# A hybrid attention layer on one core: PSUM banks, one engine's additions, paces and rings in six small edits

## The chip, the core and the metric

The kernel runs on one core of a Trainium2 chip. The metric is device time in microseconds (us) of one execution. Three runs of the kernel before gave 2157.15, 2158.1 and 2159.87 us, median 2158.1 us.

## The reference, cut to what matters

All in float32, 2048 tokens of 1024 features, behind 16 meta tokens:

```
xn = rms_norm(h);  proj = xn @ w_in                    # 6400 columns
sb_q, sb_k, sb_v, sw_q, sw_k, sw_v, sb_z, sw_z, g_sb, g_sw = split(proj)
o_sb = stick_breaking_attention(sb_q, sb_k, sb_v)      # 8 heads of 64, all earlier tokens
o_sw = sliding_window_attention(rope(sw_q), rope(sw_k), sw_v, sinks)   # 16 heads, 2 kv heads, window 128
y_sb = (o_sb * silu(sb_z)) @ w_branch_sb
y_sw = (o_sw * silu(sw_z)) @ w_branch_swa
h = h + (sigmoid(g_sb) * y_sb + sigmoid(g_sw) * y_sw) @ w_out
out = rms_norm(h) * final_norm_gain
```

Stick-breaking weights are products of `1 - sigmoid(score)` along the keys. The kernel forms them as a running product (a scan on VectorE) and takes differences of values in place of differences of weights.

## The kernel before

Each float32 operand of a large product is split into a high part and a low remainder (both of the type float32r), and a product is three matmuls: high by high, low by high, high by low. Tokens go in four groups of 512 (`g`), handled as two halves: groups 2 and 3, then 0 and 1 (the tokens are stored in reverse).

The stages of a half: **window**, in which the main stream on TensorE projects 128 columns at a time (`col_tile`, `gemm`, L403 to L405) while a side stream (`attend`) does the window attention; **stick**, in which the main stream projects gates (sigmoid on ScalarE, L567) while the side stream (`stick`) does stick-breaking; then the last gates. After both halves **finish** does the branch projections (`project`, L223 to L225), the merge, the output projection (L282 to L284) and the final norm.

TensorE's instructions are in the order of the code. `weave` sets how main and side alternate: each piece of the main stream gives credit by a `ratio`, and each piece of the side stream yields its cost. `SR` (L32) multiplies the window's ratio; a yield of 0.45 (L932) is the price of one stick row. The other engines' order, and that of the DMA queue on SyncE (SP), is made by the framework's scheduler, save at the start, where some of them are written out by hand.

PSUM is held in named rings of banks: `g` 2, `z` 2, `t` 2, `zm` 1, `o` 1. SBUF scratch comes from rings too: `tmp` (7 tiles of 128x512), and in finish `a` (6), `R` (32) and `L` (32).

In `stick`, `row` makes scores in `z` (and `zm`, for the block that holds the meta keys), takes a sigmoid on ScalarE (L869), masks on GpSimd (L871), and scans on VectorE (L873). `turn` transposes finished weights into `t` (L886), and `evac_split` copies them out: ScalarE the high part (L112), then VectorE the remainder (L113). `turn_meta` does the same for the meta keys through `zm` (L896), and ScalarE copies the high part there once more (L899). `values` accumulates a head's output in `o` (L915), 128 rows, of which the two halves are to be added. At the end of a head and group ScalarE copies 64 rows to `tmp` (L919), and VectorE adds the other 64 from the bank (L920). The meta keys' product stays in `zm` (L911) until VectorE has added it for a pair of heads (L922).

In `window`, `rope` rotates a projected tile: four copies of 32 rows on ScalarE (L627, L628), two products on VectorE (L629, L630), and their sum on GpSimd (L631). `put_k` and `put_q` split the result (L639 to L641, L688, L689). The attention's turned weights are split by L112 and L113, masked on GpSimd (L741), multiplied in `o` (L754), and added up by L756 and L760. Its exponentials are L716.

Helpers named below: `firsts` (L528) turns the first column of each value tile, through `zm`; `meta_cols` (L426) turns a small meta tile, by default through `zm`; `sb_k`'s `later` first loads such a tile from DRAM (`msd`) and then turns it through `t`. `split` makes high and low weights (L108 on GpSimd, L109 on GpSimd or VectorE). `gated` loads two tiles, multiplies them (L197), and splits the product (L199 ScalarE, L200 VectorE). In finish, `out_weights` loads and splits a tile of `w_out` (L234, L235).

Of the kernel before, what the change touches and what calls it, by code (L numbers as in the profile page):

```python
# [31 lines left out]
SR = 1.05  # L32
# [12 lines left out]
def tile_kernel(ctx, tc, x, xt, meta, metat, gain, w_in, w_sb, w_sw, w_out, sinks, fgain,  # L45
# [146 lines left out]
    def gated(src, zz, k, g, ring, stg):  # L192

        a, b = stg(), stg()
        DMA(a, src[k][g])
        DMA(b, zz[k][g])
        V.tensor_tensor(a, a, b, op=ALU.mult)  # L197
        h, l = ring(), ring()
        A.copy(h, a)  # L199
        V.tensor_tensor(l, a, f32(h), op=ALU.subtract)  # L200
        return h, l

    def finish(ringl, osw, first):
# [6 lines left out]
        def ringr(dt=F32R):  # L210
            return cp.tile([P, GT], dt, tag="R", name="ringr", bufs=32)
# [5 lines left out]
        DMA(fg, fgain.to_broadcast([P, D]))  # L217

# [8 lines left out]
        for half, groups in enumerate(halves):  # L227
            part, merged, wo = {}, {}, {}

            def out_weights(k, ch):  # L230
                raw = small("a", AB)
                DMA(raw, w_out[0, k * P:(k + 1) * P, ch * GT:(ch + 1) * GT])
                h, l = wo[k, ch] = ringr(), ringr()
                A.copy(h, raw)  # L234
                V.tensor_tensor(l, raw, f32(h), op=ALU.subtract)  # L235
# [4 lines left out]
            for d, g in order:  # L240
                if d == 4 and g == groups[0]:
                    if half == 0:
                        cp.tile([P, 48], F32, name="padr")
                    osb = {(k, g): gated(od, zs, k, g, ringr, lambda: small("a", AB)) for g in groups for k in range(4)}
# [7 lines left out]
                part[d, g] = ringr(F32)  # L252
# [14 lines left out]
            for g in groups:  # L267
                for t0 in range(0, 4, 2):
                    res, ssq = {}, {}
                    end = (half, g, t0) == (1, groups[1], 2)  # L270
                    for ch in range(2):
                        cs = slice(ch * GT, (ch + 1) * GT)
                        for t in (t0, t0 + 1):
# [25 lines left out]
                    for t in (t0, t0 + 1):  # L299
# [23 lines left out]
                if half == 0:  # L323
                    g2 = halves[1][g - groups[0]]
                    osw2.update({(k, g2): gated(ow, zw, k, g2, ringl, lambda: small("a", AB)) for k in range(8)})
# [111 lines left out]
    spare = [False]  # L437

# [4 lines left out]
    def sb_k(p):  # L443
        def use(g, acc, ms):
# [4 lines left out]
            if ms is not None:  # L449
                def later():  # L450
                    if p < 2:
                        t = tp.tile([NM, P], F32, tag="ms", name="ms", bufs=2)
                        DMA(t, msd[p])
                    mc = meta_cols(t if p < 2 else ms, "t" if p < 2 else "zm")
# [45 lines left out]
    def sb_v(p):  # L500

        def use(g, acc, ms):
# [22 lines left out]
            def firsts():  # L525

                tr = ps("zm")
# [75 lines left out]
    def window(half, groups, sp):  # L603
# [20 lines left out]
        def rope(acc, c, s, t, u, scale):  # L624
# [6 lines left out]
            G.tensor_tensor(t, t, u, op=ALU.add)  # L631
# [14 lines left out]
        def sw_k():  # L646
            def use(g, acc, ms):
# [142 lines left out]
    def stick(groups, bp, sums_of={}):  # L790
# [102 lines left out]
        def turn_meta(h, g):  # L893
            tr = ps("zm")
# [4 lines left out]
            A.copy(w[64:96], tr[:32])  # L899
            av_todo.append((h, g, vm[:, h // 2, :], w, None, False, False))  # L900

        def values():
# [6 lines left out]
            if wl is None:  # L909
                st["m"] = ps("zm")  # L910
# [334 lines left out]
```

## Time and profile before

| what | value |
|---|---|
| median of three runs | 2158.1 us |
| the profiled execution's own time | 2158.47 us |
| its span, first to last instruction | 2156.8 us |
| VectorE busy | 1359.7 us (63%) |
| ScalarE busy | 1025.2 us (48%) |
| GpSimd busy | 376.2 us (17%) |
| GB/s over the span | 176 |

A row of a group reads: line, engine, operation, tiles written and read, shape, count, then busy time and mean duration, then the idle time of that engine before these instructions and what ended it. A row of the waits reads: engine, tile and line, what it waited for, total, number of times, longest. PE is TensorE, PEld its weight load, DVE VectorE, ACT ScalarE, POOL GpSimd.

### The profile page before, as it was taken

The page shows a single profiled execution, that of the slowest core. Times are in us where ns is not written, and L with a number is a line of the kernel's source. Part 1 is how long each engine was busy: PE and PEld are TensorE (multiplying, and loading weights), DVE is VectorE, ACT ScalarE, POOL GpSimd, SP SyncE. Part 2 cuts the span into 40 slices and gives each one's busy share as a digit, 9 for nine tenths or more (in the row PEclk, how much of TensorE's full clock was granted, in tenths as well). Part 3 has the DMA queues.
Part 4 walks back from the last instruction along what each step waited for, and adds up shares of the span by engine and source line. Part 5 has one row for each costly group of instructions (what it writes and reads, how often), then busy time and mean ns, then how long its engine had stood idle before and what let it go on. Part 6 is the DMA issues. An engine that isn't in the chain of part 4 may idle for free.

```text
span 2156.8 us, 30229 instructions
## 1 busy us (share of the span) xinstructions
PE 2118.4 (98%) x10534; PEld 1754.4 (81%) x10534; DVE 1359.7 (63%) x2121; ACT 1025.2 (48%) x2456; POOL 376.2 (17%) x490
## 2 busy tenths in 40 slices
PE   8899999999999999999999999999999999999998
PEld 7778887888888888888887888888888888787887
DVE  7787876465545443777746888878775446454453
ACT  6576775344444434777744555555554201221121
POOL 2233343323223200222310000000000232000000
PEclk9999999999999999999999999999999999999999
DMA  9755454755655464444355333323322985468532
GB/s 339 257 181 196 157 188 165 261 192 202 200 189 179 163 226 156 147 167 138 136 183 175 118 118 117 117 88 119 119 84 99 353 315 186 160 223 295 161 103 88
DMA packets 174520, 380.40 MB, mean 176 GB/s; under 512 B 22720, under 2 KB 40960, under 8 KB 174368
## 3 DMA queue, kind: packets, MB, share of 16 engines
q1 hardware_dynamic: 174368, 378.48, 52.2%
q8 instruction: 83, 1.36, 0.3%
q14 instruction: 69, 0.57, 0.1%
HBM read 237.35 MB, written 140.98 MB: 175 GB/s over the span
## 4 chain that ended last, share of the span: by engine, by line
PE 86%; issue 4%; DVE 4%; ACT 3%; DMA 2%; POOL 1%; SPq 0%; POOLq 0%; ACTq 0%; DVEq 0%
PE ps_g L403 14%; PE ps_g L404 14%; PE ps_g L405 14%; PE ps_o L915 6%; PE ps_z L866 5%; PE ps_t L886 5%; PE ps_z L708 3%; PE ps_o L754 3%; PE ps_g L224 1%; PE ps_g L225 1%; PE ps_g L223 1%; PE ps_z L225 1%; PE ps_z L224 1%; PE ps_z L223 1%; PE ps_t L225 1%
## 5 line engine op out<-in xcount | busy, mean ns | idle before, releaser
L403 PE MATMUL ps_g<-xh,wh 128*128 128x512 f32 x1544 | 635.2, 411 | 7.4 <-ACT xh L967 6.9
L405 PE MATMUL ps_g<-xh,wl 128*128 128x512 f32 x1544 | 606.9, 393 | 0.6 <-DVE wl L109 0.6
L404 PE MATMUL ps_g<-xl,wh 128*128 128x512 f32 x1544 | 606.8, 393 | 0.0
L873 DVE TENSOR_TENSOR_SCAN row<-row 128x512 f32<-128x512 f32 (+2 forms) x320 | 374.7, 1173 | 178.8 <-POOL row L871 109.8
L405 PEld LDWEIGHTS ps_g<-xh,wl 128*128 128x128 f32 x1544 | 290.7, 188 | 66.3 <-DVE wl L109 1.1
L403 PEld LDWEIGHTS ps_g<-xh,wh 128*128 128x128 f32 x1544 | 291.8, 189 | 53.8 <-ACT xh L967 6.9
L404 PEld LDWEIGHTS ps_g<-xl,wh 128*128 128x128 f32 x1544 | 292.4, 189 | 43.4 <-DVE xl L968 1.3
L869 ACT ACTIVATE row<-ps_z 128x512 f32<-128x512 f32 (+2 forms) x320 | 164.9, 516 | 196.2 <-PE ps_z L866 193.3
L113 DVE SCALAR_TENSOR_TENSOR wtl<-ps_t,wth 128x512 fp32r<-128x512 f32 (+1 forms) x320 | 189.7, 593 | 43.2 <-ACT wth L112 42.1
L112 ACT ACTIVATE wth<-ps_t 128x512 fp32r<-128x512 f32 (+1 forms) x320 | 170.3, 532 | 71.1 <-PE ps_t L886 69.8
L866 PE MATMUL ps_z<-kt,q 128*128 128x512 f32 (+4 forms) x640 | 177.8, 353 | 0.4 <-ACT row L869 0.4
L886 PE MATMUL ps_t<-ident,row 128*128 128x128 f32 x1088 | 171.3, 272 | 1.3 <-DVE row L873 1.3
L886 PEld LDWEIGHTS ps_t<-ident,row 128*128 128x128 f32 x1088 | 136.1, 140 | 37.5 <-DVE row L873 1.7
L871 POOL TENSOR_SCALAR_AFFINE_SELECT row<-row 128x128 f32<-128x128 f32 x128 | 42.9, 336 | 628.6 <-ACT row L869 596.9
L866 PEld LDWEIGHTS ps_z<-kt,q 128*128 128x128 f32 x640 | 118.8, 188 | 24.1 <-ACT row L869 0.8
L915 PE MATMUL ps_o<-wth,vc 128*128 128x512 f32 (+1 forms) x320 | 126.0, 394 | 4.7 <-DVE xs L920 4.5
L108 POOL TENSOR_SCALAR wh<-raw 128x1024 fp32r<-128x1024 f32 (+1 forms) x63 | 68.6, 1089 | 303.1 <-PE ps_g L404 188.6
L716 ACT ACTIVATE sc<-sc,nm 128x129 f32<-128x129 f32 x256 | 100.0, 393 | 39.8 <-DVE nm L714 39.2
L567 ACT ACTIVATE tmp<-ps_g 128x512 f32<-128x512 f32 x112 | 67.0, 598 | 108.8 <-PE ps_g L405 99.0
L915 PE MATMUL ps_o<-wtl,vc 128*128 128x512 f32 (+1 forms) x320 | 116.5, 364 | 0.0
L109 POOL TENSOR_TENSOR wl<-raw,wh 128x1024 fp32r<-128x1024 f32 (+1 forms) x43 | 97.4, 2266 | 3.1
L631 POOL TENSOR_TENSOR tmp<-tmp 128x512 f32<-128x512 f32 (+1 forms) x37 | 48.7, 1316 | 201.7 <-DVE tmp L630 75.0
(309 smaller groups left out, 3411.7 us busy)
## 6 DMA issues: line engine op xcount, KB each, us to landing
wh<-h_in_w_in SPq DMA_DIRECT2D x66, 512.0 KB
wl<-l_in_w_in SPq DMA_DIRECT2D x66, 512.0 KB
raw<-in_w_in SPq DMA_DIRECT2D x50, 512.0 KB
h_in_w_in<-wh SPq DMA_DIRECT2D x50, 512.0 KB
l_in_w_in<-wl SPq DMA_DIRECT2D x50, 512.0 KB
q<-qd SPq DMA_DIRECT2D x128, 128.0 KB
vc<-vd SPq DMA_DIRECT2D x48, 256.0 KB
kd<-tmp SPq DMA_DIRECT2D x32, 256.0 KB
```

The costliest lines, as they stand in the source:

```text
L109: (V if vsplit[0] else G).tensor_tensor(l, src, f32(h), op=ALU.subtract)
L112: A.activation(h, acc, AF.Copy, scale=scale)
L113: V.scalar_tensor_tensor(l, acc, scale, f32(h), op0=ALU.mult, op1=ALU.subtract)
L403: T.matmul(acc, lhsT=wh[:, k, :], rhs=xh[g][:, k, :], start=k == 0, stop=False)
L404: T.matmul(acc, lhsT=wh[:, k, :], rhs=xl[g][:, k, :], start=False, stop=False)
L405: T.matmul(acc, lhsT=wl[:, k, :], rhs=xh[g][:, k, :], start=False, stop=k == KT - 1)
L716: A.activation(sc[:, hh, :], sc[:, hh, :], AF.Exp, bias=nm[:, hh:hh + 1], accum_out=den[:, hh:hh + 1])
L866: T.matmul(acc[:, :b - a], lhsT=lq, rhs=kt[h][:, k0 + a:k0 + b], start=t == 0, stop=t == 1)
L869: A.activation(r[:, a:b], acc[:, :b - a], AF.Sigmoid, scale=-1.0)
L873: V.tensor_tensor_scan(r[:, :w], r[:, :w], r[:, :w], last[j] if n else 1.0, op0=ALU.mult, op1=ALU.min)
L886: T.transpose(tr[:, j * P:(j + 1) * P], rows_of[h, g, n - (j > i), j][:, k0:k0 + P], ident)
L915: T.matmul(o[:, :n], lhsT=v, rhs=r, start=first and r is wh, stop=last and r is wl)
```

## The change

Six things change; the matmuls stay the same in number and shape.

1. **Banks of stick-breaking copied out at once.** ScalarE copies all 128 rows of `o`, and VectorE adds the two halves from that copy. The product in `zm` is copied to a `tmp` tile right behind its matmul.
2. **The rotation's sum** goes from GpSimd to VectorE.
3. **Turns in other banks.** `firsts`, `turn_meta` and the meta columns of the rotated keys use `t`; `turn_meta`'s second copy reads SBUF. The two `msd` tiles are loaded when the queue of held work is refilled, ahead of the function that turns them.
4. **Paces.** The window's factor is 1.05 in the first half and 1.09 in the second. The first six rows of stick-breaking cost 1.0 in place of 0.45. In the second half a one-column exponential stands behind the preparation of the last tokens.
5. **Finish's rings.** `R` becomes two rings of 16, one for the partial sums and the first column half of `w_out`, one for the gated values and the second half. The first four row blocks of each half go 3 and 1 in place of 2 and 2.
6. **Gating in two steps.** The remainder of one tile is taken behind the product of the next.

```diff
-SR = 1.05
+SR = (1.05, 1.09)
...
-    def gated(src, zz, k, g, ring, stg):
+    def gated(src, zz, keys, ring, stg):
...
+            V.tensor_tensor(a, a, b, op=ALU.mult)
+            h, l = out[k, g] = ring(), ring()
+            A.copy(h, a)
+            if rest:
+                V.tensor_tensor(rest[0], rest[1], f32(rest[2]), op=ALU.subtract)
+            rest = l, a, h
...
-        def ringr(dt=F32R):
-            return cp.tile([P, GT], dt, tag="R", name="ringr", bufs=32)
+        def ringr(n, dt=F32R):
+            return cp.tile([P, GT], dt, tag=f"R{n}", name="ringr", bufs=16)
...
-                h, l = wo[k, ch] = ringr(), ringr()
+                h, l = wo[k, ch] = ringr(ch), ringr(ch)
...
-                for t0 in range(0, 4, 2):
+                for ts_ in ((0, 1, 2), (3,)) if g == groups[0] else ((0, 1), (2, 3)):
...
+    def load_held():
+        for p in range(2):
+            held_ms[p] = tp.tile([NM, P], F32, tag="msh", name="msh", bufs=2)
+            DMA(held_ms[p], msd[p])
+        pending.extend(held)
...
-                tr = ps("zm")
+                tr = ps("t")
                 T.transpose(tr[:8, :P], vf[:, f0:f0 + 8], ident)
...
-            G.tensor_tensor(t, t, u, op=ALU.add)
+            V.tensor_tensor(t, t, u, op=ALU.add)
...
-                        rope(meta_cols(ms), cm, sm, t, u, 1.0)
+                        rope(meta_cols(ms, "t"), cm, sm, t, u, 1.0)
...
         def turn_meta(h, g):
-            tr = ps("zm")
+            tr = ps("t")
...
-            A.copy(w[64:96], tr[:32])
+            A.copy(w[64:96], f32(w[0:32]))
...
-                st["m"] = ps("zm")
-                T.matmul(st["m"], lhsT=v, rhs=wh, start=True, stop=True)
+                acc = ps("zm")
+                T.matmul(acc, lhsT=v, rhs=wh, start=True, stop=True)
+                st["m"] = tmp()
+                A.copy(st["m"], acc)
...
-                t, both = tmp(rows=64), pair(h, g)[1]
-                A.copy(t, o[64:128])
-                V.tensor_tensor(both[64 * a:64 * a + 64], o[0:64], t, op=ALU.add)
+                t, both = tmp(), pair(h, g)[1]
+                A.copy(t, o)
+                V.tensor_tensor(both[64 * a:64 * a + 64], t[0:64], t[64:128], op=ALU.add)
...
-                yield 0.45
+                yield 0.45 if s > LT else 1.0
...
+                A.activation(tp.tile([P, 4], F32, tag="nwt", name="nwt", bufs=2)[:, :1], xl[groups[1]][:, 0, 0:1], AF.Exp, scale=0.0)
                 drain(by_group(ts, groups[:1]), by_group(ts, groups[1:]))
...
-            weave(main, side, 4 * 2.15 / 20.8 * SR)
+            weave(main, side, 4 * 2.15 / 20.8 * SR[half])
```

Line numbers in the rows of the changed kernel are its own. **Start of stick-breaking in the second half, on TensorE.** Before, where L866 is a row's score matmul, L886 a turn, and L403 to L405 one step of the main stream's projection:

```order
L866 MATMUL ps_z<-kt,q_12181 128x512
L866 MATMUL ps_z<-kt,q_12182 128x512
L866 MATMUL ps_z<-kt,q_12181 128x512
L866 MATMUL ps_z<-kt,q_12182 128x512
L866 MATMUL ps_z<-kt,q_12181 128x512
L866 MATMUL ps_z<-kt,q_12182 128x512
L403 MATMUL ps_g<-xh,wh 128x512
L404 MATMUL ps_g<-xl,wh 128x512
L405 MATMUL ps_g<-xh,wl 128x512
L866 MATMUL ps_z<-kt,q_12181 128x512
L866 MATMUL ps_z<-kt,q_12182 128x512
```

In the changed kernel a score matmul is L876, and the projection L409 to L411:

```order
L876 MATMUL ps_z<-kt,q_12199 128x512
L876 MATMUL ps_z<-kt,q_12200 128x512
L409 MATMUL ps_g<-xh,wh 128x512
L410 MATMUL ps_g<-xl,wh 128x512
L411 MATMUL ps_g<-xh,wl 128x512
L876 MATMUL ps_z<-kt,q_12199 128x512
L876 MATMUL ps_z<-kt,q_12200 128x512
L409 MATMUL ps_g<-xh,wh 128x512
L410 MATMUL ps_g<-xl,wh 128x512
L411 MATMUL ps_g<-xh,wl 128x512
```

One projection step now stands between any two of the first rows; before, three rows stood in a line.

**End of stick-breaking in the second half, on TensorE.** Before, with the meta turn L896, the meta product L911 and the heads' products L915:

```order
L896 MATMUL ps_zm<-ident,xs 32x128 x4
L403 MATMUL ps_g<-xh,wh 128x512
L404 MATMUL ps_g<-xl,wh 128x512
L405 MATMUL ps_g<-xh,wl 128x512
L886 MATMUL ps_t<-ident,row 128x128 x4
L915 MATMUL ps_o<-wth,vc 128x512
L915 MATMUL ps_o<-wtl,vc 128x512
L403 MATMUL ps_g<-xh,wh 128x512
L404 MATMUL ps_g<-xl,wh 128x512
L405 MATMUL ps_g<-xh,wl 128x512
```

In the changed kernel the meta turn is L906, a turn L896, the meta product L921 and the heads' products L927:

```order
L906 MATMUL ps_t<-ident,xs 32x128 x4
L896 MATMUL ps_t<-ident,row 128x128 x4
L927 MATMUL ps_o<-wth,vc 128x512
L927 MATMUL ps_o<-wtl,vc 128x512
L927 MATMUL ps_o<-wth,vc 128x512
L927 MATMUL ps_o<-wtl,vc 128x512
L921 MATMUL ps_zm<-wm_71,vm 128x512
L927 MATMUL ps_o<-wth,vc 128x512
L927 MATMUL ps_o<-wtl,vc 128x512
L409 MATMUL ps_g<-xh,wh 128x512
```

The last turns and products now stand without projection steps between them.

**A head's end in the second half's stick-breaking, on ScalarE.** Before, L919 being the copy from `o`, L869 the rows' sigmoid, L112 the turned weights' high part:

```order
L112 ACTIVATE wth<-ps_t 128x512
L869 ACTIVATE row<-ps_z 128x512
L112 ACTIVATE wth<-ps_t 128x384
L567 ACTIVATE tmp<-ps_g 128x512
L919 COPY tmp<-ps_o 64x512
L869 ACTIVATE row<-ps_z 128x512
```

In the changed kernel L923 is the copy from `zm`, L931 the one from `o`, L879 the rows' sigmoid:

```order
L112 ACTIVATE wth<-ps_t 128x512
L879 ACTIVATE row<-ps_z 128x512
L112 ACTIVATE wth<-ps_t 128x384
L923 COPY tmp<-ps_zm 128x512
L931 COPY tmp<-ps_o 128x512
L879 ACTIVATE row<-ps_z 128x512
```

One more copy stands directly ahead of the one that empties `o`; the gate's sigmoid has moved away from there.

More of the change, by code (lines that the diff above doesn't have):

```diff
@@ L190, in rings @@
         return lambda dt=F32R: lp.tile([P, GT], dt, tag="L", name="ringl", bufs=32)
-    def gated(src, zz, k, g, ring, stg):
[L194 to L201, printed above, removed]
+    def gated(src, zz, keys, ring, stg):
+        out, rest = {}, None
+        for k, g in keys:
+            a, b = stg(), stg()
+            DMA(a, src[k][g])
+            DMA(b, zz[k][g])
+            V.tensor_tensor(a, a, b, op=ALU.mult)
[4 more added lines that the diff above has]
+            rest = l, a, h
+        if rest:
+            V.tensor_tensor(rest[0], rest[1], f32(rest[2]), op=ALU.subtract)
+        return out
     def finish(ringl, osw, first):
@@ L217, in finish @@
         DMA(fg, fgain.to_broadcast([P, D]))
+        small("gt", 3), ringr(0), ringr(1)
+        cp.tile([P, 48], F32, name="padr")
         def project(acc, ws, ox):
@@ L241, in finish @@
                 if d == 4 and g == groups[0]:
-                    if half == 0:
-                        cp.tile([P, 48], F32, name="padr")
-                    osb = {(k, g): gated(od, zs, k, g, ringr, lambda: small("a", AB)) for g in groups for k in range(4)}
+                    osb = gated(od, zs, [(k, g) for g in groups for k in range(4)], lambda: ringr(1), lambda: small("a", AB))
                 if d not in ws_of:
@@ L251, in finish @@
                 DMA(gt, gw[d][g])
-                part[d, g] = ringr(F32)
+                part[d, g] = ringr(0, F32)
                 V.tensor_tensor(part[d, g], acc, gt, op=ALU.mult)
@@ L324, in finish @@
                     g2 = halves[1][g - groups[0]]
-                    osw2.update({(k, g2): gated(ow, zw, k, g2, ringl, lambda: small("a", AB)) for k in range(8)})
+                    osw2.update(gated(ow, zw, [(k, g2) for k in range(8)], ringl, lambda: small("a", AB)))
             osw = osw2
@@ L450, in later @@
                 def later():
[L451 to L454, printed above, removed]
+                    mc = meta_cols(held_ms[p] if p < 2 else ms, "t" if p < 2 else "zm")
                     h, l = tmp(F32R)[:, :NM], tmp(F32R)[:, :NM]
@@ L1188, in tile_kernel @@
                     drain(tiles_by_tile([mk], groups))
[L1189 to L1190 removed]
+                osw.update(gated(ow, zw, todo[:4], ringl, tmp))
                 del todo[:4]
[L1192 to L1193 removed]
+            osw.update(gated(ow, zw, todo, ringl, tmp))
     first = weights(0, w_sw)
```

13 lines of the change are left out of this document (5 added, 8 removed).

## Prediction

> **What bounds the kernel now.** I read the page's first part, then TensorE's waits, then the timeline at each of them.
>
> ```profile
> PE 2118.4 (98%) x10534; PEld 1754.4 (81%) x10534; DVE 1359.7 (63%) x2121; ACT 1025.2 (48%) x2456; POOL 376.2 (17%) x490
> ```
>
> TensorE is the bound nearly everywhere, and the change leaves its 10534 matmuls alone. Only what it waits for can go:
>
> ```profile
> PE ps_g L403 <- ACT xh L967: 6.9, 1, 6.9
> PE ps_o L915 <- DVE xs L920: 4.5, 12, 0.8
> PE ps_zm L866 <- DVE xs L922: 2.8, 3, 1.4
> PE ps_zm L528 <- DVE vt L113: 2.7, 2, 1.7
> PE ps_zm L426 <- DVE vv L113: 2.3, 1, 2.3
> PE ps_o L754 <- DVE os L760: 2.0, 2, 1.0
> PE ps_t L426 <- DMA ms<-msd: 1.7, 1, 1.7
> PE ps_t L886 <- DVE row L873: 1.3, 2, 0.8
> PE ps_z L282 <- ACT ringr L234: 1.3, 1, 1.3
> ...
> PE ps_z L708 <- DVE sc L712: 0.6, 1, 0.6
> PE ps_g L223 <- ACT ringl L199: 0.6, 1, 0.6
> ...
> PE ps_g L403 <- DVE tmp L629: 0.4, 1, 0.4
> PE ps_z L866 <- ACT row L869: 0.4, 1, 0.4
> ```
>
> The first row is the load before the first matmul and stays. Each of the others here is a place that the change touches. A wait costs more than its idle time, as one in the timeline of the second half's stick-breaking shows:
>
> ```profile
> 1536.18 0.58 ACT L919 COPY tmp<-ps_o 64x512 f32<-64x512 f32 x1
> 1536.73 0.39 PE L404 MATMUL ps_g<-xl,wh 128*128 128x512 f32 x1
> 1536.80 0.68 DVE L920 TENSOR_TENSOR xs<-ps_o,tmp 64x512 f32<-64x512 f32 x1 [0.83 <-ACT tmp L919]
> 1536.96 0.40 PE L405 MATMUL ps_g<-xh,wl 128*128 128x512 f32 x1
> 1537.54 0.50 PE L915 MATMUL ps_o<-wth,vc 128*128 128x512 f32 x1 [0.18 <-DVE xs L920]
> 1537.87 0.40 PE L915 MATMUL ps_o<-wtl,vc 128*128 128x512 f32 x1
> ```
>
> Matmuls start 0.23 us apart (1536.73 to 1536.96). Here the next two starts are 0.58 and 0.33 later, 0.45 more than two steps, for 0.18 of idle time: each wait costs 0.27 us of refilling besides. I add that to every wait.
>
> **The change part by part**, against the profiled execution's 2158.47 us (0.4 above the median of the runs).
>
> *Banks copied out.* In these rows ScalarE has read its half of `o` at 1536.76, but TensorE, ready at 1537.19, waits for VectorE's addition until 1537.48. A copy of all 128 rows frees the bank at 1536.76, since one instruction takes 0.58 us by its 512 columns. So the 12 waits go: 4.5 + 12 x 0.27 = 7.7. `zm` is freed behind its matmul instead of behind L922: 2.8 + 3 x 0.27 = 3.6. Against that, in one head of two the new copy from `zm` (0.58 us like L919) stands ahead of the one from `o`, more than the margin of 0.43: 0.15 + 0.27 late, 0 to 16 times, so 0 to 6.7. VectorE's additions now hold nobody. The meta turn's place in `t` is priced by its own copies:
>
> ```profile
> 1650.82 0.60 PE L896 MATMUL ps_zm<-ident,xs 128*32 128x128 f32 x4
> 1651.46 0.59 ACT L112 ACTIVATE wm<-ps_zm 32x512 fp32r<-32x512 f32 x1 [1.00 <-PE ps_zm L896]
> 1652.08 0.68 DVE L113 SCALAR_TENSOR_TENSOR wm<-ps_zm,wm 32x512 fp32r<-32x512 f32 x1 [0.89 <-ACT wm L112]
> ```
>
> The bank is free 1.94 us after the turn began, and of two banks it is wanted two turns on; only where VectorE is late does anybody wait, 0 to 16 x 0.3 us. I take 0.5 for either: gain 11.3 - 1.0 = **10.3**.
>
> *Other turns.* `firsts` and the rotated meta keys no longer queue behind `zm`'s evacuation: 2.7 + 2.3 + 3 x 0.27 = 5.8. The longest of them, 2.3 us ending at 90.75, is followed by this:
>
> ```profile
> 91.00:94.50 3.50, 3.50 (x9) 2.68 (x10) 2.54 (x5) 1.91 (x7) 1.08 (x1) 0.54 1.03 421
> ```
>
> The granted clock is 0.54 for 3.5 us: 3.5 x 0.46 = 1.6 us lost, which goes with the wait. The Trainium skill (TensorE: Matmul & The Clock Gate, What's actually happening) has the clock halve after an idle window of about 3.4 us; by that, a wait of 2.3 us needn't be the cause, this 1.6 would stay, and the sum would be 1.6 smaller. The trace has the dip right behind the wait and behind none of the shorter ones, so I keep it. What takes the waits' place is VectorE:
>
> ```profile
> 112.00:160.00 48.00, 44.83 (x245) 37.37 (x244) 42.16 (x82) 36.69 (x109) 15.22 (x19) 1.00 0.52 176
> 160.00:360.00 200.00, 199.96 (x1076) 167.76 (x1074) 158.11 (x297) 138.36 (x409) 73.04 (x103) 1.00 0.51 177
> ```
>
> Between 112 and 160 it is busy 42.2 of 48 us, and both `firsts` waits lie there. With four rotation sums more (2.7 us) in 45 us it would be full, so half of these two waits (3.2 with refills) comes back: gain 5.8 + 1.6 - 1.6 = **5.8**.
>
> *Meta tiles loaded ahead:* 1.7 + 0.27, **2.0**. The two small loads stand one projected tile earlier in SP's queue, and TensorE doesn't want what is behind them there.
>
> *Rotation's sum.* What it replaces, its likeness on VectorE, and how the two engines meet:
>
> ```profile
> L631 POOL TENSOR_TENSOR tmp<-tmp 128x512 f32<-128x512 f32 (+1 forms) x37 | 48.7, 1316 | 201.7 <-DVE tmp L630 75.0 <-DMA qd<-tmp 71.1 <-ACT sc L711 16.1
> L630 DVE TENSOR_TENSOR tmp<-tmp,sn 128x512 f32<-128x512 f32 x14 | 9.6, 682 | 0.0
> 93.42 1.28 POOL L631 TENSOR_TENSOR tmp<-tmp 128x512 f32<-128x512 f32 x1 [7.10 <-DVE tmp L630]
> 93.45 1.27 DVE L630 TENSOR_TENSOR tmp<-tmp,mcs 128x16 f32<-128x16 f32 x1
> ```
>
> 37 sums of 0.68 us are 25 us for VectorE in place of 49 for GpSimd. The last two rows show what that buys back: a 16-column product lasts 1.27 us, as long as GpSimd's sum beside it. In 160 to 360 eleven sums bring VectorE from 79% to (158.1 + 7.5) / 200 = 83%, and TensorE waits nowhere there (199.96 busy). So the cost is 0 to 25 us; hidden while `z`, `g` and `t` are emptied in time. I take **-1**.
>
> *Paces.*
>
> ```profile
> 871.69 1.28 ACT L716 ACT_TABLE_LOAD   x1
> 1102.79 1.28 ACT L567 ACT_TABLE_LOAD   x1
> 1109.49 0.47 PE L754 MATMUL ps_o<-ph,vv 128*128 128x512 f32 x1 [0.95 <-DVE os L760]
> ```
>
> The exponential's table is loaded at 871.69, ahead of the first window unit; TensorE's waits for L712 and L629 follow. The early exponential takes it out of the way: 0.6 + 0.4 + 2 x 0.27 = 1.5. The load then stands in ScalarE's queue ahead of casts of the last tokens, to which TensorE comes three projections (3 x 24 x 0.23 = 16.6 us) later. At 1102.79 a gate's sigmoid comes between exponentials and costs a load; with 1.09 the side stream ends before the gates. But the first half has the same wait for L760 with no such load, so I count half of 0.95 + 0.27 plus small slips: 0.8. First rows one by one: L886 1.3, L866 0.4, three refills, 2.5; with one projection step to a row they come 5 x 0.23 = 1.15 us apart, and a row's turn follows five rows later, so these go. The 6 x 0.55 of pace come due at the end, where nothing is left between the last turns and products: TensorE has eight transposes and four products, about 1.8 us, between the meta turn's start and its product, which needs 0.64 + 0.59 + 0.58 for ScalarE's two copies at least and another 0.6 for the turn between them, and then the last turn's remainder. About 1.0 us in each half, 0 to 2. Sum 1.5 + 0.8 + 2.5 - 2.0 = **2.8**.
>
> *Finish.*
>
> ```profile
> 1845.93 8.49 SPq L55 DMA_DIRECT2D a<-in_w_out  x8
> 1852.03 1.93 ACT L234 CAST ringr<-a 128x512 fp32r<-128x512 f32 x3 [4.53 <-DMA a<-in_w_out]
> ```
>
> The second column half of `w_out` is asked for at 1845.93, converted from 1852.03, and wanted at 1851.25. Three row blocks ahead of it in place of two move the wish by 24 x 0.23 = 5.5 us: 1.3 + 0.27 = 1.6 go. The fourth block's input must wait for the first block's output, with six banks to cover that. Gating in two steps frees VectorE from ScalarE's copy, but that wait (0.6 + 0.27) hangs on DMAs in six `a` tiles: half, 0.4. **2.0.**
>
> Sum: 10.3 + 5.8 + 2.0 - 1 + 2.8 + 2.0 = 21.9; 2158.5 - 21.9 = 2136.6, less 0.4 for the median, **2136 us**. With nothing given back and every wait gone whole it is 11.3 + 7.4 + 2.0 + 5.2 + 2.5 = 28.4, so 2130.
>
> **The rivals.** *The finer edits miss* (0.12): the 1.09, the rings and the gating change no wait, and the clock dip stays: 2136 + 0.8 + 2.0 + 1.6 = 2140.
>
> *GpSimd holds the new additions* (0.13). In the first half's stick-breaking GpSimd is busy 29.5 of 100 us:
>
> ```profile
> 500.00:600.00 100.00, 100.00 (x516) 83.38 (x515) 57.71 (x73) 44.73 (x112) 29.45 (x30) 1.00 0.57 190
> 453.65 2.42 POOL L109 TENSOR_TENSOR wl<-raw,wh 128x1024 fp32r<-128x1024 f32 x1
> 453.79 3.36 DVE L873 TENSOR_TENSOR_SCAN row<-row 128x512 f32<-128x512 f32 x1
> ```
>
> The scan there takes 3.36 us beside GpSimd's 2.42. The 32 head sums read `o` and SBUF before; now they read SBUF twice, as the scan does. If each of the 16 of the first half that meet GpSimd were held for half of such a run, and TensorE waited for what stands behind, in 29.5% of the cases: 16 x 0.3 x 1.2 = 5.8, so 2142. The Trainium skill says so too (GPSIMD Engine Reference, Specifications): GpSimd's SBUF interfaces are shared with VectorE, which contends when it has two SBUF inputs. The rows agree.
>
> *The waits change their name* (0.14): `o` and `t` are then waited for behind ScalarE's longer queue and VectorE's remainders. The bounds above, 6.7 and 4.8 in place of 1.0, with the `firsts` waits back in full (1.6 more): 2136 + 10.5 + 1.6 = 2148.
>
> *No change* (0.07): that and the misses together, about 2154.
>
> *VectorE becomes the bound of the windows, slower* (0.04): every rotation sum delays an emptied bank by its 0.68 and a refill, 36 x 0.95 = 34: 2136 + 1 + 33 = 2170. It decides from where VectorE is full; 83% speaks against it, 112 to 160 for it.
>
> **How the numbers follow.** My forecast holds 0.50, from 2130 to 2139. The range takes in the next three cases, 2140 to 2148: 2130 to 2148. A measurement of this kernel tells 0.2%, 4.3 us, from none. Faster 0.50 + 0.12 + 0.13 + 0.14 = 0.89, the same 0.07, slower 0.04.
>
> **What would show it.** TensorE's waits should lack L920, L922, L528, L426 and the `msd` load, and the clock at 91 to 95 should be full. VectorE should be busy over 95% between 110 and 155. New waits of about a microsecond should stand at the two ends of stick-breaking. I am wrong if the windows show many short waits for L712, L629 or L113, or if `t` in stick-breaking does.

## The result and the profile after

The changed kernel takes 2136.47 us (median of four executions, 2134.13 to 2137.47) against 2157.7 us for the kernel before: a ratio of 0.9898, with a 95% interval of 0.9881 to 0.9915. That is 21.2 us less. The profiled execution took 2136.89 us with a span of 2135.0, so 21.8 us of span went. In the runs that follow, one execution of the kernel with fast first rows (2387 us) and one of the kernel before (2336 us) ran at a granted clock of 0.83 and 0.85, and the times given are medians without these two.

The page's row of busy time answers to the one shown of the kernel before: VectorE and ScalarE do a little more, GpSimd less, and TensorE the same 10534 matmuls in a shorter time.

```profile
PE 2112.2 (99%) x10534; PEld 1755.9 (82%) x10534; DVE 1383.4 (65%) x2158; ACT 1030.5 (48%) x2471; POOL 333.1 (16%) x453
```

TensorE's waits in the changed kernel (engine, tile and line, what it waited for, total us, times, longest). The lines have moved: L896 is now the turn in `t`, L921 and L927 are the products of stick-breaking in `zm` and `o`, L527 a turn of value tiles in `zm`, L232 a matmul of finish's projection, and L203 the deferred subtraction of gating.

```profile
PE ps_g L409 <- ACT xh L979: 7.0, 1, 7.0
PE ps_g L232 <- DVE ringl L203: 1.9, 1, 1.9
PE ps_o L409 <- ACT xh L383: 1.6, 1, 1.6
PE ps_t L896 <- DVE wtl L113: 1.2, 2, 0.6
PE ps_z L718 <- DVE q L699: 0.8, 2, 0.5
PE ps_o L927 <- DVE wtl L113: 0.7, 1, 0.7
PE ps_t L896 <- DVE wm L113: 0.7, 1, 0.7
PE ps_zm L527 <- DVE vt L113: 0.5, 1, 0.5
```

The twelve waits of `o` for an addition, the three of `zm`, those of `firsts`, of the rotated meta keys and for the `msd` load, and the ones in the window for a rotation are all gone. What is left is the load at the start, the wait at 66.9 us for the first group's tokens (it was 0.96 us before, and lies between nothing and 1.6 from kernel to kernel in what follows, without any edit near it), three short waits in the windows (two of L718 behind a query's remainder, one of L527), a few at the two ends of stick-breaking, and one that is *larger* than before: L232, in finish, at 1926.8 us.

Stretches of the changed kernel (from and to, length, busy time of PE, PEld, DVE, ACT and POOL with counts, granted clock, DMA share, GB/s):

```profile
69.00:72.50 3.50, 3.27 (x13) 2.48 (x13) 3.06 (x6) 3.39 (x7) 0.00 (x0) 0.57 1.02 413
90.50:94.00 3.50, 3.50 (x29) 2.96 (x28) 2.33 (x7) 2.17 (x8) 0.00 (x0) 1.00 0.94 378
112.00:155.00 43.00, 42.47 (x236) 35.90 (x235) 40.16 (x81) 35.16 (x105) 10.08 (x16) 1.00 0.49 165
153.00:353.00 200.00, 199.84 (x1076) 167.47 (x1074) 163.28 (x309) 140.26 (x410) 62.98 (x95) 1.00 0.51 179
1929.40:1933.00 3.60, 3.60 (x11) 2.73 (x10) 2.67 (x6) 1.24 (x2) 0.00 (x0) 0.55 0.89 290
```

The half clock behind the old 2.3 us wait is gone (90.5 to 94 is at 1.00). But two new stretches of it stand behind the two longest waits that remain after the load at the start: at 69, and at 1929.4 behind the wait of gating, where 3.6 us at 0.55 lose another 1.6 us. VectorE is busy 40.16 of 43 us between 112 and 155 (93%) and 163.28 of 200 in the steady window (82%).

### The profile page after: what moved, and what is told of

It reads as the page before. It is cut to its first block, busy times and chain, and to the rows that moved or that the text cites. A ratio compares the mean times of both kernels' runs of the same rounds, so it can differ in the third digit from the quotient of the medians.

```text
span 2135.0 us, 30157 instructions
## 1 busy us (share of the span) xinstructions
PE 2112.2 (99%) x10534; PEld 1755.9 (82%) x10534; DVE 1383.4 (65%) x2158; ACT 1030.5 (48%) x2471; POOL 333.1 (16%) x453
## 4 chain that ended last, share of the span: by engine, by line
PE 85%; issue 7%; DMA 3%; DVE 2%; ACT 1%; SPq 1%; POOL 0%; POOLq 0%; DVEq 0%; ACTq 0%
PE ps_g L409 15%; PE ps_g L411 14%; PE ps_g L410 14%; PE ps_o L927 5%; PE ps_t L896 4%; PE ps_z L876 4%; PE ps_z L718 3%; PE ps_o L764 3%; PE ps_g L232 1%; PE ps_g L233 1%; PE ps_z L231 1%; PE ps_z L233 1%; PE ps_z L232 1%; PE ps_g L231 1%; PE ps_t L747 1%
## 5 line engine op out<-in xcount | busy, mean ns | idle before, releaser
L409 PE MATMUL ps_g<-xh,wh 128*128 128x512 f32 x1544 | 634.6, 411 | 7.0 <-ACT xh L979 7.0
L411 PE MATMUL ps_g<-xh,wl 128*128 128x512 f32 x1544 | 605.9, 392 | 0.0
L883 DVE TENSOR_TENSOR_SCAN row<-row 128x512 f32<-128x512 f32 (+2 forms) x320 | 375.6, 1175 | 157.9 <-POOL row L881 105.8
L411 PEld LDWEIGHTS ps_g<-xh,wl 128*128 128x128 f32 x1544 | 290.2, 188 | 65.5 <-DVE wl L109 0.3
L409 PEld LDWEIGHTS ps_g<-xh,wh 128*128 128x128 f32 x1544 | 291.3, 189 | 52.7 <-ACT xh L979 7.0
L879 ACT ACTIVATE row<-ps_z 128x512 f32<-128x512 f32 (+2 forms) x320 | 165.0, 516 | 192.0 <-PE ps_z L876 191.3
L112 ACT ACTIVATE wth<-ps_t 128x512 fp32r<-128x512 f32 (+1 forms) x320 | 170.5, 533 | 71.8 <-PE ps_t L896 68.9
L876 PE MATMUL ps_z<-kt,q 128*128 128x512 f32 (+4 forms) x640 | 178.2, 353 | 0.0
L896 PE MATMUL ps_t<-ident,row 128*128 128x128 f32 x1088 | 171.1, 272 | 1.9 <-DVE wtl L113 1.2
L896 PEld LDWEIGHTS ps_t<-ident,row 128*128 128x128 f32 x1088 | 135.7, 140 | 39.1 <-DVE wtl L113 2.3
L876 PEld LDWEIGHTS ps_z<-kt,q 128*128 128x128 f32 x640 | 118.9, 188 | 23.2
L927 PE MATMUL ps_o<-wth,vc 128*128 128x512 f32 (+1 forms) x320 | 125.1, 391 | 0.0
L108 POOL TENSOR_SCALAR wh<-raw 128x1024 fp32r<-128x1024 f32 (+1 forms) x63 | 68.2, 1082 | 336.1 <-PE ps_g L410 209.5
L927 PE MATMUL ps_o<-wtl,vc 128*128 128x512 f32 (+1 forms) x320 | 116.9, 365 | 0.7 <-DVE wtl L113 0.7
L109 POOL TENSOR_TENSOR wl<-raw,wh 128x1024 fp32r<-128x1024 f32 (+1 forms) x43 | 100.5, 2337 | 3.3
L270 ACT CAST ringl<-gt 128x512 fp32r<-128x512 f32 x32 | 20.0, 624 | 152.3 <-DVE gt L268 144.6
```

Source lines behind the costliest of these rows:

```text
L109: (V if vsplit[0] else G).tensor_tensor(l, src, f32(h), op=ALU.subtract)
L112: A.activation(h, acc, AF.Copy, scale=scale)
L409: T.matmul(acc, lhsT=wh[:, k, :], rhs=xh[g][:, k, :], start=k == 0, stop=False)
L411: T.matmul(acc, lhsT=wl[:, k, :], rhs=xh[g][:, k, :], start=False, stop=k == KT - 1)
L876: T.matmul(acc[:, :b - a], lhsT=lq, rhs=kt[h][:, k0 + a:k0 + b], start=t == 0, stop=t == 1)
L879: A.activation(r[:, a:b], acc[:, :b - a], AF.Sigmoid, scale=-1.0)
```

## The experiments

Unless it is said otherwise a kernel is compared with the kernel before, in executions on the same chip; the ratio's 95% interval stands in brackets. Where a kernel is compared with the changed kernel, the two were not run side by side; each has executions of the kernel before beside it, whose median differs by 0.6 us at most (2157.4 to 2158.0).

### The banks of stick-breaking alone

```diff
+                acc = ps("zm")
+                T.matmul(acc, lhsT=v, rhs=wh, start=True, stop=True)
+                st["m"] = tmp()
+                A.copy(st["m"], acc)
...
-                t, both = tmp(rows=64), pair(h, g)[1]
-                A.copy(t, o[64:128])
-                V.tensor_tensor(both[64 * a:64 * a + 64], o[0:64], t, op=ALU.add)
+                t, both = tmp(), pair(h, g)[1]
+                A.copy(t, o)
+                V.tensor_tensor(both[64 * a:64 * a + 64], t[0:64], t[64:128], op=ALU.add)
```

> The kernel before with only the copies of o and zm in stick-breaking. Theory that each part gives the waits it removes: the waits for L920 and L922 (4.5 and 2.8 us) go with their refills, 10.8 of 11.3 us, so about 2147; the list of TensorE's waits then lacks both and keeps all others. Rival, waits change their name: a third to a half comes back as waits for o behind ScalarE or for t, about 2151 to 2153.

Measured: 2146.72 us, ratio 0.9949 [0.9936, 0.9961], 10.9 us less. TensorE's waits in this kernel begin so; the two rows of L920 and L922, which stood between these, are gone, and no row for a copy stands in their place:

```profile
PE ps_g L403 <- ACT xh L969: 6.9, 1, 6.9
PE ps_zm L528 <- DVE vt L113: 2.7, 2, 1.7
```

Most others of that list stay as they were. One doesn't: the wait of L282 for `w_out` (1.3 us in the kernel before) has no row here, though this edit doesn't touch its code; the section on finish's rings comes back to that.
This edit is half of the whole gain. Fifteen waits with 7.3 us of idle time brought 10.9, which agrees with the price per wait (idle time and 0.27 us of refilling: 11.3), but the interval, 8 to 14 us, is too wide to measure that price.

### The other turns and the meta tiles alone

```diff
-                tr = ps("zm")
+                tr = ps("t")
                 T.transpose(tr[:8, :P], vf[:, f0:f0 + 8], ident)
...
-                        rope(meta_cols(ms), cm, sm, t, u, 1.0)
+                        rope(meta_cols(ms, "t"), cm, sm, t, u, 1.0)
...
-                pending.append(lambda: pending.extend(held))
+                pending.append(load_held)
```

> The kernel before with only the turns of firsts and of the rotated meta keys in bank t, and the two meta tiles loaded ahead (the meta turn of stick-breaking stays in zm). Theory: the waits of L528, L426 for VectorE and L426 for the load go, 5.8 + 2.0, the half clock at 91 to 94.5 goes too, 1.6, and half of two waits comes back, 1.6: about -7.8, so 2150. Rival, the clock dip has nothing to do with that wait: the dip stays and the time is about 2152. Rival, VectorE bounds the stretch: the waits come back whole further on, about 2156.

Measured: 2151.61 us, 0.9970 [0.9959, 0.9981], 6.0 us less. In this kernel's waits the three rows of L528 and L426 are gone. Two smaller ones have come, and a stretch far away that was at full clock is now at half:

```profile
PE ps_g L403 <- DVE tmp L633: 1.2, 2, 0.8
...
PE ps_zm L521 <- DVE vt L113: 0.8, 1, 0.8
```

```profile
1532.60:1536.00 3.40, 3.40 (x11) 2.90 (x12) 1.61 (x2) 1.15 (x4) 0.00 (x0) 0.55 0.20 77
```

One of the two waits for L633 (0.8 us, at 92.1) and the one at 135.7 for VectorE's remainder follow where the removed ones had hidden VectorE's lag: 1.6 us and two refills come back. The stretch at 1532.6 stands behind the wait for L926 of 1.37 us at 1531, which the kernel before had too (1.38 us), there with no dip behind it. So the dip at 91 went in this profiled execution and another came, and the time, between the theory's 2150 and the 2152 of the rival that lets the dip stay, doesn't decide between them.

### The rotation's sum alone, and the change without it

```diff
-            G.tensor_tensor(t, t, u, op=ALU.add)
+            V.tensor_tensor(t, t, u, op=ALU.add)
```

> The kernel before with only the rotation's sum on VectorE. Theory: hidden work, VectorE's busy time up by 20 to 25 us and GpSimd's down by 45 to 49, TensorE's waits the same within 1 us, 2157 to 2159. Rival, it is the sum's latency that made the early waits: the waits of L405 for wl and L426 for vv around 84 to 91 go with it, 2153 to 2155. Rival, VectorE becomes the bound: waits for L712, L689 or L113 appear in the windows, 2162 or more.

Measured: 2155.28 us, 0.9990 [0.9981, 0.9998], 2.3 us less. My expectation of a small cost has failed. The rival, that the sum's latency counts, has held in its mechanism, at the edge of its size (2153 to 2155). The place is the longest wait of the window's head. First the timeline of the kernel before, from the sum to the casts that need it:

```profile
84.18 2.14 POOL L631 TENSOR_TENSOR tmp<-tmp 128x512 f32<-128x512 f32 x1 [5.62 <-issue]
...
86.35 2.54 ACT L639 CAST kk<-tmp 64x512 fp32r<-64x512 f32 x4 [6.96 <-POOL tmp L631]
```

Then the same with the sum on VectorE, on to TensorE's wait:

```profile
83.46 0.67 DVE L631 TENSOR_TENSOR tmp<-tmp 128x512 f32<-128x512 f32 x1
...
84.17 2.54 ACT L639 CAST kk<-tmp 64x512 fp32r<-64x512 f32 x4 [5.08 <-DVE tmp L631]
...
88.58 0.23 PE L426 MATMUL ps_zm<-ident,ms 16*128 16x16 f32 x1 [1.74 <-DVE vv L113]
```

The four casts L639 wait for the sum, and behind them in ScalarE's queue stands the copy that empties `zm`. GpSimd's sum took 2.14 us there, VectorE's 0.67. TensorE's wait falls from 2.29 to 1.74 us, its wait of 0.6 us for L109 at 85 is gone, and the clock behind the longer wait stays whole, as this kernel's stretch shows (the last section tells why the shorter wait alone doesn't explain that):

```profile
90.50:94.00 3.50, 3.19 (x26) 2.51 (x25) 2.87 (x8) 2.17 (x7) 0.00 (x0) 1.00 0.21 83
```

Against that, a wait of 0.8 us for VectorE comes new at L517. The opposite edit, the changed kernel with the sum on GpSimd again:

> The changed kernel with the rotation's sum on GpSimd again. Theory, hidden work at either place: within 1.5 us of the changed kernel, 2135 to 2138, the two waits for q L699 (0.8 us) gone, VectorE 23 us less busy. Rival, the move is what lets the earlier turns' gain stand: waits reappear between 84 and 155, 2139 to 2142.

Measured: 2138.8 us, 0.9911 [0.9898, 0.9925], 2.3 us more than the changed kernel, between the theory (up to 2138) and the rival (from 2139, with waits between 84 and 155). Among the waits that the changed kernel doesn't have are these; the last two end at 91.5 and 84.0, in the rival's stretch:

```profile
PE ps_o L764 <- DVE os L770: 0.9, 1, 0.9
PE ps_g L409 <- DVE tmp L639: 0.8, 1, 0.8
PE ps_g L411 <- DVE wl L109: 0.6, 1, 0.6
```

Both directions give the same 2.3 us. The intervals of the changed kernel and of this one overlap (0.9881 to 0.9915 against 0.9898 to 0.9925), so the second is told by the traces more than by the times. The wait of the first half's window end for L770 (L760 in the kernel before) is gone with the sum on VectorE and the rest of the change, and comes back when only the sum goes back. The timelines suggest a way, which no run tests: with the sums on it GpSimd makes a high part of weights (L108) at 345.78 behind a second mask, in the changed kernel at 344.26 ahead of it, and VectorE, whose subtraction L109 waits 0.61 us for that, is late at the window's last addition.

### The paces alone, and with the first rows fast

```diff
-SR = 1.05
+SR = (1.05, 1.09)
...
-                yield 0.45
+                yield 0.45 if s > LT else 1.0
...
+                A.activation(tp.tile([P, 4], F32, tag="nwt", name="nwt", bufs=2)[:, :1], xl[groups[1]][:, 0, 0:1], AF.Exp, scale=0.0)
...
-            weave(main, side, 4 * 2.15 / 20.8 * SR)
+            weave(main, side, 4 * 2.15 / 20.8 * SR[half])
```

> The kernel before with only the paces and the early exponential. Theory: the waits for L712 and L629 at 877, one of two for L760, and the three for L873 and L869 at the start of the second half's stick-breaking go, 4.8, and two tails of about 1.0 to 1.6 us each come instead: -2 to -3, so about 2155. Rival, only the table loads matter: -2.5 with the start's waits staying. Rival, the tails take all of it: 2157 to 2158.

Measured: 2152.65 us, 0.9976 [0.9966, 0.9986], 4.8 us less. Waits of this kernel, and the stretch behind the first row's longer wait:

```profile
PE ps_zm L911 <- ACT wm L899: 3.1, 2, 2.5
...
PE ps_o L915 <- DVE xs L920: 2.3, 7, 1.0
```

```profile
748.60:752.00 3.40, 3.40 (x10) 2.62 (x9) 1.50 (x6) 3.33 (x5) 1.20 (x6) 0.50 0.02 5
```

The tails cost 3.1 us of idle time and a dip of the clock, more than I had counted. What makes up for it was not among my terms: with the rows shifted against the main stream, `o`'s waits fall from 12 (4.5 us) to 7 (2.3 us), and `zm`'s for L922 from 2.8 us to 0.4. The change takes these same waits by its copies, so this part of the 4.8 us is not there to be had twice. The same kernel with all rows at 0.45:

```diff
-                yield 0.45 if s > LT else 1.0
+                yield 0.45
```

> The kernel before with the two factors and the early exponential, but all rows of stick-breaking at 0.45. Theory from the run of the changed kernel with fast first rows: the slow first rows bring no net gain, since what they take off the start they give back at the tails, so this kernel is as fast as the one with all the paces or up to 3 us faster: 2150 to 2153 us, with the start's waits (L886, L866) there and the tails' wait for wm absent. Rival, the slow rows are what made the paces worth 4.8 us: then 2155 to 2157.

Measured: 2154.86 us, 0.9986 [0.9978, 0.9995], 3.1 us less, between the two expectations; its interval overlaps that of the kernel with all the paces. Its waits show `o` about as in the kernel before, and the second half's window end without its wait for L760 (one time is left of two, the first half's):

```profile
PE ps_o L915 <- DVE xs L920: 4.0, 11, 0.8
...
PE ps_o L754 <- DVE os L760: 1.2, 1, 1.2
...
PE ps_z L708 <- DVE sc L712: 0.5, 1, 0.5
PE ps_z L708 <- DVE q L689: 0.5, 1, 0.5
```

The last two rows were not expected. The early exponential has taken the table load away from the head of the second half's window, and the wait for L712 is there still, at 877 (0.6 us before), so the load was not what made TensorE wait for it. The wait for L629 there is gone, and one for L689 has come later in that window. L282 has no row here either.

And the changed kernel with all rows at 0.45, by the same line:

> The changed kernel with the first six rows of stick-breaking at 0.45 again. Theory: the start's waits come back, 2.5 less the 0.8 that the changed kernel still has there, and the tails' 2.7 us go: no net change, 2135 to 2137, with the waits at other places. Rival, the slow start also serves the turns behind it: 2138 or more.

Measured: 2130.32 us, 0.9876 [0.9861, 0.9891], some 6 us less than the changed kernel. The expectation of no net change has failed. Its gating wait:

```profile
PE ps_g L232 <- DVE ringl L203: 1.1, 1, 1.1
```

The start's waits are back (1.3 us for L883 and 0.3 for the sigmoid), and the tails' rows (L921, L927, and L896 for `wm`) are gone. The gating wait happens to be 1.1 us in place of 1.9, with a full clock behind it. So slow first rows do not pay in the changed kernel, but this run doesn't tell their own cost from that of the dip which they happened to lead to. The runs with gating in one step that follow do, as far as the noise lets them.

### Gating in one step

The changed kernel with the remainder taken at once:

```diff
             A.copy(h, a)
-            if rest:
-                V.tensor_tensor(rest[0], rest[1], f32(rest[2]), op=ALU.subtract)
-            rest = l, a, h
-        if rest:
-            V.tensor_tensor(rest[0], rest[1], f32(rest[2]), op=ALU.subtract)
+            V.tensor_tensor(l, a, f32(h), op=ALU.subtract)
```

> The changed kernel with gating in one step again. Theory after the result: the deferred remainder frees the a tile later, its refill falls behind a gt load in SP's queue that waits for a bank, and TensorE waits 1.9 us at 1926 and runs at half clock behind it. With one step the wait is at most the 0.8 us of the kernel before and the dip goes: 2.5 to 3.5 us faster than the changed kernel, 2133 to 2134. Rival, as I had predicted: two steps help by 0.4, so one step costs 0 to 1 us, 2136.5 to 2137.5, and the wait at 1926 has another cause and stays.

Measured: 2132.39 us, 0.9887 [0.9873, 0.9900], 4.1 us less than the changed kernel (2132.07 to 2134.73 us in four executions against 2134.13 to 2137.47; the intervals of the two ratios overlap). To see why, first the timeline of the changed kernel before its wait (start, duration, engine, line, tiles; in brackets the idle time and what ended it; SPq is the DMA queue):

```profile
1922.98 0.32 SPq L55 DMA_DIRECT2D gt<-gw  x1
...
1923.20 0.69 DVE L199 TENSOR_TENSOR a<-a 128x512 f32<-128x512 f32 x1 [0.25 <-DMA a<-zw]
...
1923.92 0.32 SPq L55 DMA_DIRECT2D a<-zw  x1
...
1925.28 0.62 ACT L201 CAST ringl<-a 128x512 fp32r<-128x512 f32 x1 [0.67 <-DVE a L199]
...
1927.34 0.69 DVE L199 TENSOR_TENSOR a<-a 128x512 f32<-128x512 f32 x1 [1.54 <-DMA a<-zw]
1927.95 0.68 DVE L203 TENSOR_TENSOR ringl<-a,ringl 128x512 fp32r<-128x512 f32 x1
...
1928.68 0.50 PE L232 MATMUL ps_g<-ringl,wh 128*128 128x512 f32 x1 [1.87 <-DVE ringl L203]
```

Then the same place with gating in one step, and the clock behind it:

```profile
1919.49 0.32 SPq L55 DMA_DIRECT2D a<-zw  x1
...
1925.42 0.50 PE L227 MATMUL ps_g<-ringl,wh 128*128 128x512 f32 x1 [0.55 <-ACT ringl L201]
```

```profile
1927.00:1930.40 3.40, 3.40 (x16) 2.78 (x15) 2.74 (x5) 1.17 (x3) 0.00 (x0) 1.00 0.95 322
```

In one step the last `zw` tile is asked for at 1919.49, 5.4 us before TensorE stops (1925.42 - 0.55 = 1924.87). In two steps it is asked for at 1923.92, 2.9 us before TensorE stops (1926.81). A load is asked for when a tile of the ring `a` comes free. The load of `gt` ahead of it in the queue, which the expectation named, doesn't hold it: that one has gone out at 1923.30, and what the `zw` load waits for is the product L199, which ends at 1923.89 and had waited for a `zw` load itself. The deferred subtraction holds its `a` tile until the next tile's product has run, so in two steps the last load gets its tile from a later product. TensorE then waits not for the tile of that load but for the remainder of the tile before. The high part of that tile is ready at 1925.90 (1925.28 + 0.62), but its remainder, L203 at 1927.95, stands in VectorE's order behind the product that waits for the load. So two steps free VectorE from ScalarE's copy, but they take one tile of lead from the loads and put a finished tile behind the next tile's load. The wait grows from 0.55 to 1.87 us, and the longer one has a clock dip of 1.6 us behind it: 1.3 + 1.6 = 2.9 of the 4.1 us. The rest is within what the two intervals leave open; the changed kernel's profiled execution also has the longer wait at 66.9 with its dip, which this edit doesn't touch.

### Finish's rings and row blocks alone

```diff
-        def ringr(dt=F32R):
-            return cp.tile([P, GT], dt, tag="R", name="ringr", bufs=32)
+        def ringr(n, dt=F32R):
+            return cp.tile([P, GT], dt, tag=f"R{n}", name="ringr", bufs=16)
...
-                for t0 in range(0, 4, 2):
+                for ts_ in ((0, 1, 2), (3,)) if g == groups[0] else ((0, 1), (2, 3)):
```

> The kernel before with the rings of finish by use and the first row blocks 3 and 1, gating left in one step. The prediction's step: the wait of L282 for L234's conversion at 1851 (1.3 us and a refill) goes, 1.6 us, so about 2155.9 us, with no new wait of TensorE in finish. Rival, the fourth block's input has to wait for the first block's output: a wait in the output projection of 1 us or more takes its place, and the time is that of before.

Measured: 2155.79 us, 0.999 [0.9981, 1.0], 2.2 us less; from the times alone it can barely be told from no change. In its waits L282 has no row any more, and none has come for the fourth block's input. But that doesn't show that the rings did it. Five kernels above have the old rings and the old row blocks and lack other parts of the change: in three of them (the banks, the rotation's sum, the paces with fast rows) L282 has no row either, and in the other two it waits 0.3 and 0.2 us. The load and its first conversion in the last of these, the kernel with all the paces:

```profile
1841.19 7.35 SPq L55 DMA_DIRECT2D a<-in_w_out  x8
...
1846.07 0.62 ACT L234 CAST ringr<-a 128x512 fp32r<-128x512 f32 x1 [3.44 <-DMA a<-in_w_out]
```

Here the first tile is converted 4.9 us after it is asked for. In the kernel before, by the rows in the prediction, it was 6.1 us. So the 1.3 us seem to be for the most part one slow load in one profiled execution. The new order gives such a load more room, but whether that is worth anything is not shown. The start of this kernel shows something else, which the last section reads.

### The better version

The changed kernel with gating in one step, and with the six slow rows booked in the side stream's planned cost, so that the end of stick-breaking no longer outlasts the main stream:

```diff
-            cost_sb = 8 * sum(4 * (4 - g) for g in groups) * 1.31 + 8 * 0.75
+            cost_sb = 8 * sum(4 * (4 - g) for g in groups) * 1.31 + 8 * 0.75 + 6 * 0.55
```

> The changed kernel with gating in one step, and with the six rows' added price put into the sum from which the side stream's ratio is made, so that it ends before the main stream. Theory: 2.5 to 3.5 us for the gating and its clock dip, 2.7 for the two tails: 2130 to 2132. Rival, the tails only move to the head of the next stage or the steeper ratio makes the middle wait: 2133 to 2135.

Measured: 2129.6 us, 0.9869 [0.9856, 0.9883], 6.9 us less than the changed kernel. Waits of this kernel in stick-breaking and in gating:

```profile
PE ps_t L892 <- DVE wtl L113: 1.0, 2, 0.6
...
PE ps_g L227 <- ACT ringl L201: 0.6, 1, 0.6
```

Both tails are gone, and behind the gating wait the clock stays whole. The other way to get rid of the tails is to leave the rows fast, with gating in one step:

> The changed kernel with gating in one step and all rows of stick-breaking at 0.45. If the two corrections are separate, 2131.7 minus what gating in one step brought beyond the lost clock dip: the gating wait falls from 1.1 to 0.6 us, so about 2131. If the dip that was absent with fast rows counts to the gating, as in the other run, the same 2131. With the first rows at 1.0 and their cost booked at the end it was 2129.6, so this kernel should be 1 to 2 us slower than that one; rival, the two are alike within 0.5 us, and slow first rows are worth nothing even when they are paid for.

Measured: 2130.36 us, 0.9874 [0.9861, 0.9888]. The two can't be told apart, and this one has the start's waits in place of the slow rows' remainder:

```profile
PE ps_t L892 <- DVE row L879: 1.3, 2, 0.8
```

So slow first rows are worth nothing that can be measured here, even when they are paid for: the rival of that expectation. Left unpaid they cost some 2 us, 2132.39 against 2130.36, again with intervals that overlap. The same kernel with gating in two steps took 2130.32 us: with fast first rows, where the gating wait of 1.1 us has no dip behind it, one step or two makes no difference that can be measured. The 4.1 us are thus the price of two steps beside the slow rows, with a dip, and not of two steps as such. Both versions of this section beat the kernel before by some 28 us, and the changed kernel by 6 to 7.

## Why the prediction was right, and where its terms were not

The forecast of 2136 stands 0.5 us from the 2136.47 measured. That is closer than its terms deserve: two of them had the wrong sign, and they cancelled, and two others, the paces and the rings, rest in part on waits that the runs do not bear out. The table sets each term beside what its part did by itself, against the kernel before, save for gating, which was undone in the changed kernel, beside its slow first rows. Parts measured apart needn't add up: that they come to 22.1 us beside the 21.2 of the whole is partly chance, since the paces alone also took waits that the copies take.

| term of the sum | predicted gain, us | measured gain, us |
|---|---|---|
| banks copied out | 10.3 | 10.9 |
| other turns, and meta tiles ahead | 5.8 + 2.0 | 6.0 |
| rotation's sum | -1 | 2.3 |
| paces | 2.8 | 4.8 alone |
| finish's rings and blocks | 1.6 | 2.2 |
| gating in two steps | 0.4 | -4.1 |
| sum | 21.9 | 22.1 |

*Banks copied out* was right in mechanism and size. The copy of `zm` ahead of that of `o`, bounded at 6.7 us and taken at 0.5, shows no row of waits. The meta turn in `t`, also taken at 0.5, shows one wait that can be read (L896 for `wm`, 0.7 us); no run has that turn by itself.

*Other turns.* The waits went as said, and the dip at 91 with them, which by the last section is in part luck. That VectorE would be full between 112 and 160 and bring half of the `firsts` waits back (1.6 us) was too much for the changed kernel, which shows 0.5 us there, with VectorE at 93% and not over 95%. In the edit by itself the 1.2 us at L403 and 0.8 at L521 came. What I had not counted in that run is a dip of the clock in another place, at 1532.6.

*The rotation's sum* is a step that failed. I priced VectorE's added work and bounded it at zero from below, since GpSimd's sum seemed to be off the path. The runs show a path through it: at the head of the first half's window a sum, its casts and the emptying of `zm` stand in one chain, and TensorE waits at its end. The bound "below nothing" that each unknown cost is owed was missing here.

*Paces.* The second half's L760 went as argued. The 1.5 us for the table load did not come: without the load at that place TensorE still waits 0.5 us for L712 there, and for the 0.4 us of L629 that went, 0.5 for L689 came. That the run without slow rows gained 3.1 us, near the 1.5 + 0.8 predicted, is luck; its traces lack L282's 1.3 us, which no pace touches. That the first half's wait for L760 would stay was wrong: the rest of the change and the rotation's sum together remove it, while with the sum alone 0.8 us of it are left. The tails came as predicted, at the meta product (L921) and the last turn's product (L927), and near the size: 0.4 + 0.7 us idle with two refills in the first half, 0.6 in the second, where 1.0 each was taken. The slow rows' 2.5 us were too much, since L896 still waits 0.6 us for `wtl` in the second half's start. Net of tails the slow rows bring nothing.

*Finish.* The rings' 1.6 us are not shown: the wait from which they were priced is missing in kernels with the old rings too, and seems to be a slow load of one execution. Gating is the other step that failed, and in sign. I wrote that the wait "hangs on DMAs in six `a` tiles", took half of it for that reason, and did not ask what deferring the subtraction does to those six tiles. It holds one of them longer, the last load goes out one tile later, and the wait triples.

Of the rivals, that *VectorE bounds the windows* falls with 82% in the steady window and full TensorE there (199.84 of 200). That *GpSimd holds the new additions* has a true mechanism and no weight, as the durations of the 32 new additions show (least, median and greatest, in ns):

```profile
L932 DVE TENSOR_TENSOR xs<-tmp x32: 686/689/2305, 424.2 to 1634.5; 64x512 f32<-64x512 f32 x32
```

Two of the 32 are held, to 2305 and 1535 ns, the longer beside a GpSimd subtraction (L109) of 2402 ns, but the others are not, and nobody waits for them since the banks are free by then. That is the point of the copies. That *the waits change their name* holds only at the ends of stick-breaking and in gating. That *the finer edits miss* was in part right: the 1.09 worked, the gating did not, and the rings show no effect of their own.

## What to carry to other kernels

On a kernel that one engine bounds, look for each buffer that the engine wants next, and let it be emptied by the first instruction that can, not by the one whose result is wanted: the two copies out of banks are half of this gain. Before an operation is deferred to free an engine, ask which buffer it holds meanwhile, and which load waits for that buffer in a queue that runs in order. And an operation on an idle engine is not off the path because that engine is idle; move it and look who waited for it. Before a wait is priced from one profile, look whether it stands in the profile of a second kernel with the same code there.

## What the hardware showed that was not expected

The clock's dips do not follow the length of the wait alone. Each dip in these traces lasts 3.41 us at half clock and costs some 1.7 us. When stretches of 3.41 us are laid end to end from the first moment of full clock on (13.26 us in the run of finish's rings), every dip fills one of them. Four such stretches of the run of finish's rings, the first with most of L426's wait of 2.26 us, the third with the whole wait for `msd` (1.54 us); then the row of that second wait in its timeline:

```profile
88.36:91.77 3.41, 1.68 (x8) 1.39 (x9) 2.11 (x5) 3.30 (x7) 0.00 (x0) 1.00 1.04 423
91.77:95.18 3.41, 3.41 (x21) 2.85 (x20) 3.35 (x7) 2.21 (x7) 1.50 (x2) 0.50 0.82 334
98.60:102.01 3.41, 1.87 (x10) 1.23 (x10) 0.17 (x1) 0.26 (x3) 0.00 (x0) 1.00 0.06 7
102.01:105.42 3.41, 3.41 (x9) 2.67 (x10) 1.97 (x7) 1.03 (x5) 1.04 (x1) 0.50 0.20 60
```

```profile
101.66 0.23 PE L426 MATMUL ps_t<-ident,ms 16*128 16x16 f32 x1 [1.54 <-DMA ms<-msd]
```

TensorE idles 1.73 us of the first stretch and 1.54 of the third, and the stretch behind each is at 0.50. In the kernel with the paces alone the same wait of L426, 2.29 us, falls on the border of two stretches:

```profile
86.44:89.85 3.41, 1.99 (x9) 1.31 (x7) 2.80 (x5) 3.30 (x6) 0.00 (x0) 1.00 1.01 408
89.85:93.27 3.42, 2.53 (x10) 1.75 (x10) 2.16 (x5) 3.01 (x9) 0.00 (x0) 1.00 1.03 420
93.27:96.68 3.41, 3.13 (x25) 2.74 (x26) 3.31 (x6) 2.45 (x7) 1.51 (x2) 1.00 0.56 228
```

It idles 1.42 us of one and 0.88 of the other, and no dip follows. Over the thirteen traces a dip followed all eight stretches with 1.73 us of idle time or more and two of the four with 1.54 to 1.66, and none with 1.52 or less. This leaves out the stretch in which a kernel's matmuls end; in one trace that one idled 1.95 us, and half clock came one stretch later. The Trainium skill (TensorE: Matmul & The Clock Gate, What's actually happening) speaks of a free-running window of about 3.4 us, and the length of the dips and their places agree with it; that a whole such window must be idle does not agree, since about half of one was enough. So my step "the dip goes with the wait" was right for a weaker reason than I gave: what counts is the idle time within one stretch, 1.5 us at the least here, and a long wait may draw a dip or not by where it falls. In the run of the rotation's sum the wait of 1.74 us fell on a border too, so that its missing dip is no gain of that edit. The first moment of full clock lies anywhere from 10.4 to 13.7 us in these traces, and executions of one kernel have mean granted clocks from 0.997 to 0.999, where one dip is 0.0008. So a dip more or less, 1.7 us, belongs to the noise of a gain of 2 us.
